# Four instead of three blocks of the up projection with seven products, and other places for the units between their steps

## The chip, the cores and the metric

The kernel runs on one core of a Trainium2 chip. The core has a matrix engine (TensorE; PE in the profile, with PEld for its weight loads), a vector engine (VectorE, DVE), a scalar engine (ScalarE, ACT), GpSimd (POOL) and SyncE (SP), each working through its own queue in order; here SP issues the loads and POOL issues the stores of the hidden layer. The metric is device time in microseconds (us) of one execution, as the median of several. Before the change it is 1566.11 us (three runs, 1565.74 to 1566.63).

## What is computed

One encoder block on 256 tokens of width 2048, in float32: a retention branch and a latent-attention branch, merged by gates and added to the residual stream, then a squared-ReLU MLP, then a last norm. The change concerns the MLP:

```python
z = _rmsnorm(h, norm_mlp_g[l]) @ w_up[l]            # 256 x 2048 times 2048 x 8192
h = h + jnp.square(jax.nn.relu(z)) @ w_down[l]      # 256 x 8192 times 8192 x 2048
```

## The kernel before, in words

**Two halves for one float32.** Each float32 operand is split into `hi`, a copy cast to fp32r by ACT, and `lo`, the remainder, which DVE gets by subtracting (`split`, L550 and L551). A product is then three matmuls: activation hi by weight hi, activation lo by weight hi, activation hi by weight lo. The activations are split once. Every weight of `w_up` is loaded by SP in pieces of 512 KB, cast by ACT, and subtracted by DVE.

**Two ways to the up projection.** The 8192 hidden columns are 64 groups of 128.

- A *unit* (class `Unit`) makes one group of 128 columns from all 2048 rows: two parts of 8 row tiles. Each part has 8 matmuls of 512 columns (L176: the activations' hi and lo halves side by side) and 8 of 256 columns (L180). Its result stands in one PSUM bank. `evict` copies it out on ACT (L1266), adds the two halves on DVE (L1267), and two parts later ACT takes the relu (L1270) and the square (L1231), and POOL stores it (L1232).
- A *block* makes 1024 columns (8 groups) in eight *steps* (class `Step`, j = 0 to 7). A step takes 256 rows by 1024 columns as a 2 by 2 arrangement of sub-blocks, and multiplies it in seven products instead of eight (`PRODUCTS`), each of three matmuls of 512 columns (L333 to L335): 21 matmuls. It has four parts, with 6, 6, 6 and 3 matmuls. Their weights are made from what was loaded: `fa` (L307), and `fb` in two adds (L316, L317), all on DVE; then part 0's weights (`ra`), part 1's (`fa`), part 2's (`fb`) and half of part 3's (`rb`) are split as above. The seven sums accumulate over the eight steps in seven PSUM banks.

At a block's end `s_end` adds the seven sums up: four copies on ACT (L522 to L528), four adds on DVE (L520) at once, and three later ones (`SUMS`), 4, 7 and 10 parts on. The result stands tokens by columns and must be turned. A *turn* (L1284) is four transposes on PE into one PSUM bank, then a relu (L1236) and a square (L1231) on ACT, and a store. A block has four turns, one at the start of part 1 of each of the next block's steps 1 to 4 (`between`). The last block's are put into two late units (`drain`).

**Banks.** There are eight PSUM banks in two rings of four (`mmps` L149, `atps` L152). During a block the seven products hold four of the one and three of the other. The fourth of the `atps` ring serves the units and the turns in turn.

**The order.** All engines follow one order written out by hand. `parts` lists the parts of steps and units. `stream` (L470) goes through it: for part n it first issues the loads up to part n + 6, then the preparation (ACT's cast, DVE's adds and subtractions) up to part n + 4, then the matmuls of part n with what follows them (a unit's `evict`, a block's `s_end`), and then what is due (`soon`). So on DVE and ACT, whatever follows the matmuls of part n stands behind the preparation of part n + 4 and ahead of that of part n + 5. Weights split by `split` live in seven slots, raw ones in five.

The first three units (`EARLY`) come before the first block, the last two (`LATE`) after the last. In the first block DVE also makes the combinations of the activations for steps 4 to 7 (`hc.make`, from part 7 and from part 24 on, `MAKE`), in four pieces each.

Where the other units stand is set by `use`, a set of (block, step, part): after such a part a unit follows.

```python
slots = [(u, j, h) for u in range(SU) for j in range(SJ) for h in (1, 3)][:-1]
whole = [t for t in slots if t[2] == 3]
room = len(units) - len(whole)
```

With three blocks there are 64 - 24 = 40 units, 35 of them between the steps. Each step but the very last is followed by one (23), and the 12 left stand in the middle, after part 1, of every second step (0, 2, 4 and 6).

The down projection then reads the hidden layer back, the units' columns first and the blocks' after, and its order follows from the number of blocks in the same way.

Of the kernel before, what the change touches and what calls it, by code (L numbers as in the profile page):

```python
# [27 lines left out]
CHUNK = 64  # L28
DFF = 8192
FT = DFF // P  # L30
SU = 3
SJ = KT // 2
ST = SU * 1024 // P
EARLY, LATE = 3, 2
AHEAD = 4
PAIRED = 6
MAKE = 7, 2 * EARLY + 18
SUMS = (4, 7, 10), (0, 1, 2)
MANUAL = {getattr(mybir.EngineType, n) for n in ('Activation', 'DVE', 'PE', 'SP', 'Pool')}
# [66 lines left out]
def block_kernel(ctx: ExitStack, tc: tile.TileContext, A):  # L106
# [50 lines left out]
    def wtile(kind, shape):  # L157
        uid[0] += 1
        dt, bufs = (F32, 5) if kind == "raw" else (F32R, 4)
        return wp.tile(shape, dt, tag=kind, bufs=bufs, name=f"{kind}{uid[0]}")  # L160
# [440 lines left out]
    for k in range(KT):  # L601
        t = lead0[:, N_VEC:] if k == 0 else wtile("raw", [P, LEAD])
# [674 lines left out]
    def turn(u, jj):  # L1277
        pT = atps(f"zt{u}{jj}")
        for j in range(2):
            kt = 2 * jj + j  # L1280
            for t in range(2):
                o = j * S + t * P
                src = zo[:, 0, 2 * t + kt // 4, kt % 4 * P : kt % 4 * P + P]
                PE.transpose(pT[:, o : o + P], src, ident)  # L1284
        square(4 * u + jj, pT)

    def step(u, j, qs):
        def end():
            sums = s_end(qs, zo[:, 0].rearrange("p (t c) n -> p t c n", t=2), zo[:, 1])
            next(sums)  # L1290
            later.extend([d, lambda: next(sums)] for d in SUMS[u == SU - 1])
            turns.extend(lambda jj=jj: turn(u, jj) for jj in range(4))
# [13 lines left out]
    early = [Unit(i, 0) for i in range(EARLY)]  # L1306
    parts = [(e, h) for h in range(2) for e in early]
    units = list(range(EARLY, FT - ST - LATE))
    slots = [(u, j, h) for u in range(SU) for j in range(SJ) for h in (1, 3)][:-1]
    whole = [t for t in slots if t[2] == 3]  # L1310
    room = len(units) - len(whole)
    halves = [t for t in slots if t[2] == 1]
    if room >= 0:
        use = set(whole) | {halves[i * len(halves) // room] for i in range(room)}
    else:
        use = {t for t in whole if t[1] != PAIRED or t[0] >= -room}
    for u in range(SU):
        qs = {}
        for j in range(SJ):
# [69 lines left out]
    def finish(half, t, c, n, lo=0, hi=512):  # L1389
        h = residual(half, t, c)[:, lo:hi]  # L1390
        ps = both[half].q[ROLE[t, c]][:, lo:hi]
        V.scalar_tensor_tensor(h, in0=ps, scalar=rh2[:, t : t + 1], in1=h, op0=ALU.mult, op1=ALU.add)

        def square():
            SC.activation(ps, h, AF.Square, accum_out=ssf[:, t, n : n + 1])

        return square
# [90 lines left out]
    with tc.manual_schedule(engines=MANUAL):  # L1488
        stream(parts, after)
        assert not later  # L1490
        for t in range(2):
            for c in range(2):
# [10 lines left out]
                else:  # L1503
                    halves = [finish(1, t, 1, 3, 0, 256)]
# [86 lines left out]
```

## Time and profile before

| what | before |
| --- | --- |
| median of three runs | 1566.11 us (1565.74 to 1566.63) |
| span of the profiled execution | 1564.8 us |
| PE, PEld busy | 1551.3 us (99%), 1311.0 us (84%) |
| DVE busy | 1316.0 us (84%) |
| ACT busy | 962.6 us (62%) |
| POOL busy | 39.3 us (3%) |
| mean granted TensorE clock | 0.998 |
| DMA | 333.70 MB, mean 213 GB/s |
| first block starts, last block ends on PE | 895.78, 1209.45 us |

The profile is of one execution, and its own time is given as the span, from the first to the last instruction; no other time is shown for that execution. The three timed runs lie 0.9 to 1.8 us above it. A row of the timeline gives start, duration, engine, line, operation, output and inputs with their shape, the count where several equal ones in a row are merged, and in brackets how long the engine had been idle before and what released it. Durations of instructions that follow each other can overlap a little, so what one costs its engine is read from start to start.

### The profile page before, as it was taken

How to read it: one execution, taken by the hardware profiler on the slowest of the kernel's cores; microseconds unless marked ns; L12 is line 12 of the kernel's file. 1: busy time of each engine (PE TensorE's matmuls, PEld its weight loads, DVE VectorE, ACT ScalarE, POOL GpSimd, SP SyncE). 2: the span in 40 equal slices, each digit the busy share in tenths (PEclk: the TensorE clock that was granted, in tenths of full speed). 3: DMA queues.
4: the chain of work that ended last, by engine and by line, in shares of the span. 5: the costliest groups of instructions: out<-in, count | busy, mean ns of one | idle time of the engine just before them, and what ended most of it. 6: DMA issues, size and time to landing. Idle time of an engine off the chain costs nothing.

```text
span 1564.8 us, 21391 instructions
## 1 busy us (share of the span) xinstructions
PE 1551.3 (99%) x7655; PEld 1311.0 (84%) x7655; DVE 1316.0 (84%) x1787; ACT 962.6 (62%) x1416; POOL 39.3 (3%) x76
## 2 busy tenths in 40 slices
PE   9999999999999999999999999999999999999997
PEld 7888888888898888888888888888888888888886
DVE  7898877799976988976567689887978899989996
ACT  6645655566545667875445567676767766656664
POOL 0000000000000000000000000000000100000000
PEclk9999999999999999999999999999999999999999
DMA  9666755566656654444556657666675977686873
GB/s 319 207 203 208 230 164 161 159 201 206 206 168 220 213 197 143 157 136 161 185 206 211 236 196 247 214 226 232 207 249 188 376 265 245 237 304 211 266 255 115
DMA packets 107626, 333.70 MB, mean 213 GB/s; under 512 B 11264, under 2 KB 12160, under 8 KB 106496
## 3 DMA queue, kind: packets, MB, share of 16 engines
q1 hardware_dynamic: 104208, 318.71, 61.1%
q0 software_dynamic: 3168, 11.54, 1.9%
q10 hardware_dynamic: 144, 2.10, 0.4%
q8 instruction: 60, 0.98, 0.3%
q14 instruction: 46, 0.38, 0.1%
HBM read 319.72 MB, written 12.58 MB: 212 GB/s over the span
## 4 chain that ended last, share of the span: by engine, by line
PE 79%; DVE 1%; issue 1%; ACT 1%; DVEq 0%; POOLq 0%; POOL 0%; ACTq 0%
PE z L176 9%; PE dn L358 7%; PE dn L359 7%; PE dn L357 7%; PE z L180 5%; PE zs L333 2%; PE zs L334 2%; PE zs L335 2%; PE mo L214 2%; PE mo L215 2%; PE mo L217 2%; PE wo L214 2%; PE wo L215 2%; PE wo L217 2%; PE gm L357 2%; PE yr L358 2%
## 5 line engine op out<-in xcount | busy, mean ns | idle before, releaser
L551 DVE TENSOR_TENSOR lo<-raw,hi 128x1024 fp32r<-128x1024 f32 (+3 forms) x214 | 232.0, 1101 | 22.7 <-ACT hi L550 22.2
L169 DVE TENSOR_TENSOR lo<-raw,hi 128x1024 fp32r<-128x1024 f32 (+1 forms) x148 | 173.2, 1171 | 89.7 <-ACT hi L168 89.6
L168 ACT CAST hi<-raw 128x1024 fp32r<-128x1024 f32 (+1 forms) x148 | 149.6, 1011 | 155.9 <-PE mo L215 44.9
L550 ACT CAST hi<-raw 128x1024 fp32r<-128x1024 f32 (+3 forms) x214 | 200.0, 953 | 55.3 <-issue 9.5
L551 DVE TENSOR_TENSOR morelo<-raw,morehi 128x1024 fp32r<-128x1024 f32 (+1 forms) x118 | 127.1, 1098 | 18.8 <-ACT morehi L550 18.3
L550 ACT CAST morehi<-raw 128x1024 fp32r<-128x1024 f32 (+1 forms) x118 | 109.1, 949 | 10.5 <-issue 3.2
L550 ACT CAST hi<-forms 128x1024 fp32r<-128x1024 f32 x70 | 73.7, 1052 | 51.2 <-DVE forms L307 28.1
L176 PE MATMUL z<-hT,morehi 128*128 128x512 f32 x408 | 101.6, 391 | 0.0
L357 PE MATMUL dn<-hi,dd 128*128 128x512 f32 x230 | 89.6, 389 | 0.0
L359 PE MATMUL dn<-hi,dd 128*128 128x512 f32 x230 | 89.5, 389 | 0.0
L358 PE MATMUL dn<-lo,dd 128*128 128x512 f32 x230 | 89.5, 389 | 0.0
L551 DVE TENSOR_TENSOR lo<-forms,hi 128x1024 fp32r<-128x1024 f32 x70 | 85.0, 1221 | 5.3 <-ACT hi L550 4.9
L176 PEld LDWEIGHTS z<-hT,morehi 128*128 128x128 f32 x408 | 74.9, 188 | 14.4
L1266 ACT COPY hs<-z 128x512 f32<-128x512 f32 x40 | 23.5, 587 | 71.2 <-PE z L180 71.1
L357 PE MATMUL dn<-morehi,dd 128*128 128x512 f32 x156 | 60.7, 389 | 0.0
L358 PE MATMUL dn<-morelo,dd 128*128 128x512 f32 x156 | 60.7, 389 | 0.0
L359 PE MATMUL dn<-morehi,dd 128*128 128x512 f32 x156 | 60.7, 389 | 0.0
L180 PEld LDWEIGHTS z<-hT,morelo 128*128 128x128 f32 x408 | 55.6, 190 | 4.0
L176 PE MATMUL z<-hT,hi 128*128 128x512 f32 x232 | 57.9, 392 | 0.0
L180 PE MATMUL z<-hT,morelo 128*128 128x256 f32 x408 | 56.9, 282 | 0.0
L307 DVE TENSOR_TENSOR forms<-raw,sraw 128x1024 f32<-128x1024 f32 x46 | 56.1, 1219 | 0.3 <-DMA raw<-w_up_s 0.3
L358 PEld LDWEIGHTS dn<-lo,dd 128*128 128x128 f32 x230 | 43.2, 188 | 9.0
(500 smaller groups left out, 4193.9 us busy)
## 6 DMA issues: line engine op xcount, KB each, us to landing
raw<-w_down SPq DMA_DIRECT2D x106, 512.0 KB, 6.0
raw<-w_up SPq DMA_DIRECT2D x80, 512.0 KB, 5.1
raw<-w_rv SPq DMA_DIRECT2D x32, 512.0 KB, 4.8
raw<-w_rg SPq DMA_DIRECT2D x32, 512.0 KB, 4.3
raw<-w_gret SPq DMA_DIRECT2D x32, 512.0 KB, 4.4
raw<-w_ret_o SPq DMA_DIRECT2D x32, 512.0 KB, 5.0
raw<-w_gmla SPq DMA_DIRECT2D x32, 512.0 KB, 4.3
raw<-w_mla_o SPq DMA_DIRECT2D x32, 512.0 KB, 3.7
```

The lines of the kernel that those rows point to most:

```text
L168: SC.copy(hi, raw)
L169: V.tensor_tensor(out=lo, in0=raw, in1=hi.bitcast(F32), op=ALU.subtract)
L176: PE.matmul(out, w[0][:, k], x.both(k0 + k), start=start and k == 0, stop=False)
L180: PE.matmul(out[:, :S], w[1][:, k], x.hi(k0 + k), start=False, stop=stop and k == n - 1)
L214: PE.matmul(out, x.hi(k0 + k, ts), w[0][:, k], start=start and k == 0, stop=False)
L215: PE.matmul(out, x.lo(k0 + k, ts), w[0][:, k], start=False, stop=False)
L217: PE.matmul(out, x.hi(k0 + k, ts), w[1][:, k], start=False, stop=stop and k == nk - 1)
L357: PE.matmul(q, ah, wh, start=start, stop=False)
L358: PE.matmul(q, ah, wl, start=False, stop=False)
L359: PE.matmul(q, al, wh, start=False, stop=self.left[f] == 0)
L550: SC.copy(hi, val)
L551: V.tensor_tensor(out=lo, in0=val, in1=hi.bitcast(F32), op=ALU.subtract)
```

## The change

`SU` goes from 3 to 4: four blocks (4096 columns) instead of three are done with seven products, and 32 groups instead of 40 as units. The slots are replaced: in each block a unit stands after part 1 of steps 1 to 6, and one after the last part of step 7, but for the last block. That makes 4 x 6 + 3 = 27 units between the steps, beside the three early and the two late ones. Within a block, steps 0 and 7 have no unit in their middle, and no unit stands between two steps.

```diff
-SU = 3
+SU = 4
 SJ = KT // 2
 ST = SU * 1024 // P
...
-PAIRED = 6
...
-    slots = [(u, j, h) for u in range(SU) for j in range(SJ) for h in (1, 3)][:-1]
-    whole = [t for t in slots if t[2] == 3]
-    room = len(units) - len(whole)
-    halves = [t for t in slots if t[2] == 1]
-    if room >= 0:
-        use = set(whole) | {halves[i * len(halves) // room] for i in range(room)}
-    else:
-        use = {t for t in whole if t[1] != PAIRED or t[0] >= -room}
+    use = {(u, j, 1) for u in range(SU) for j in range(1, SJ - 1)} | {(u, SJ - 1, 3) for u in range(SU - 1)}
     for u in range(SU):
         qs = {}
         for j in range(SJ):
             st = step(u, j, qs)
             for h in range(4):
                 parts.append((st, h))
                 if (u, j, h) in use:
                     un = Unit(units.pop(0), 0)
                     parts += [(un, 0), (un, 1)]
```

`ST`, the number of groups done in blocks, follows from `SU`, and with it the layout of the two forms of `w_up`, and the order in which the down projection takes the hidden columns.

## The prediction

> **What bounds the kernel now.** I read the page's totals first, then the stretch in which the up projection runs, block by block (a block is 1024 hidden columns, done in eight steps), then who waits for whom there, and last the rows of single instructions.
>
> ```profile
> span 1564.8 us, 21391 instructions
> PE 1551.3 (99%) x7655; PEld 1311.0 (84%) x7655; DVE 1316.0 (84%) x1787; ACT 962.6 (62%) x1416; POOL 39.3 (3%) x76
> PEclk9999999999999999999999999999999999999999
> ```
>
> TensorE is busy 99% of the span, at full granted clock. By the totals, fewer matmuls are less time. But the totals are an average, so I looked at the stage itself: the columns are stretch, length, then busy us (instructions) of PE, PEld, DVE, ACT and POOL, clock, DMA share, GB/s.
>
> ```profile
> 895.78:995.34 99.56, 99.56 (x522) 85.62 (x521) 86.57 (x99) 67.53 (x95) 7.78 (x14) 1.00 0.63 216
> 1000.90:1105.16 104.26, 104.26 (x554) 89.65 (x553) 86.75 (x96) 70.37 (x101) 8.68 (x16) 1.00 0.66 219
> 1105.16:1209.45 104.29, 104.29 (x555) 89.65 (x553) 86.37 (x97) 71.25 (x102) 8.68 (x16) 1.00 0.65 218
> ```
>
> PE never stops, DVE is already busy 83 to 87%. Where its rest lies:
>
> ```profile
> ACT hs L1266 <- PE z L180: 69.3, 34, 3.6
> DVE hs L1267 <- ACT hs L1266: 26.9, 19, 2.8
> DVE morelo L551 <- ACT morehi L550: 14.1, 21, 1.6
> ```
>
> Once per unit ACT waits for PE to finish it (L1266), and DVE waits for ACT (L1267). Both queues are in order, so they cannot prepare further than four parts beyond the unit that PE is in. DVE's free time cannot be saved up: that is the point of the whole forecast.
>
> **The change part by part. PE's saving.** The rows of PE around the end of the first block and in the next:
>
> ```profile
> 990.55 0.40 PE L333 MATMUL zs<-hi,hT 128*128 128x512 f32 x1
> ...
> 995.34 1.98 PE L176 MATMUL z<-hT,morehi 128*128 128x512 f32 x8
> ...
> 1000.90 0.40 PE L333 MATMUL zs<-morehi,hT 128*128 128x512 f32 x1
> ...
> 1009.21 0.40 PE L333 MATMUL zs<-hi,hc 128*128 128x512 f32 x1
> ...
> 1011.27 1.98 PE L176 MATMUL z<-hT,morehi 128*128 128x512 f32 x8
> ...
> 1016.83 0.40 PE L333 MATMUL zs<-hi,hT 128*128 128x512 f32 x1
> ...
> 1022.12 1.98 PE L176 MATMUL z<-hT,morehi 128*128 128x512 f32 x8
> ```
>
> A step is 990.55 to 995.34, 4.79 us for 21 matmuls (0.228 each). A unit is 995.34 to 1000.90, 5.56. Parts 2 and 3 of a step (9 matmuls) are 1009.21 to 1011.27, 2.06. A step with a turn (four transposes ahead of part 1) is 5.29, so a turn costs 0.50. The change takes out eight units and puts in eight steps and four turns: 8 x 5.56 - 8 x 4.79 - 4 x 0.50 = 4.2 us saved, all of it on the path, if PE stays fed. Bytes are the same (1 MB for a unit or a step).
>
> **What DVE is asked for.** The end of the first block on DVE:
>
> ```profile
> 991.37 0.43 DVE L1267 TENSOR_TENSOR hs<-hs 128x256 f32<-128x256 f32 x1 [0.66 <-ACT hs L1266]
> 992.32 2.36 DVE L551 TENSOR_TENSOR morelo<-raw,morehi 128x1024 fp32r<-128x1024 f32 x2 [0.52 <-ACT morehi L550]
> 994.60 1.22 DVE L307 TENSOR_TENSOR forms<-raw,sraw 128x1024 f32<-128x1024 f32 x1
> ...
> 998.20 1.22 DVE L551 TENSOR_TENSOR lo<-forms,hi 128x1024 fp32r<-128x1024 f32 x1
> 999.34 2.14 DVE L520 TENSOR_TENSOR zo<-zs,zo 128x512 f32<-128x512 f32 x3
> ...
> 1001.99 2.35 DVE L551 TENSOR_TENSOR lo<-raw,hi 128x1024 fp32r<-128x1024 f32 x2
> 1004.26 0.42 DVE L1267 TENSOR_TENSOR hs<-hs 128x256 f32<-128x256 f32 x1
> 1004.60 1.22 DVE L551 TENSOR_TENSOR lo<-forms,hi 128x1024 fp32r<-128x1024 f32 x1
> 1005.73 0.68 DVE L551 TENSOR_TENSOR morelo<-raw,morehi 128x512 fp32r<-128x512 f32 x1
> 1006.33 0.68 DVE L520 TENSOR_TENSOR zo<-zo 128x512 f32<-128x512 f32 x1
> ```
>
> From start to start: a split of 1024 takes 1.14, one of 512 0.60, part 0 of a step 3.60 (994.60 to 998.20), the four sums at a block's end 2.65, each later sum 0.61, a unit's add 0.34. So a step costs DVE 3.60 + 1.14 + 1.14 + 0.60 = 6.48 against PE's 4.79; a unit 2.27 + 0.34 = 2.61 against 5.56. Only units feed DVE's slack. Eight steps with seven units and 4.5 of sums make 74.6 on DVE, 78.8 on PE (with four turns): 95% instead of 83 to 87. On average that fits. What matters is where units stand: between the unit in step 6 and the one in step 1 of the next block lie two and a half steps with one unit, and the sums.
>
> **The boundary, summed along the queues.** T is the end of step 6's unit on PE. The rows of ACT that price its part:
>
> ```profile
> 990.75 0.59 ACT L1266 COPY hs<-z 128x512 f32<-128x512 f32 x1 [1.38 <-PE z L180]
> 991.24 2.00 ACT L550 CAST morehi<-raw 128x1024 fp32r<-128x1024 f32 x2
> 993.14 0.41 ACT L1270 ACTIVATE hs<-hs 128x256 f32<-128x256 f32 x1
> ...
> 993.91 1.04 ACT L550 CAST morehi<-sraw 128x1024 fp32r<-128x1024 f32 x1
> ...
> 1001.58 1.05 ACT L550 CAST hi<-forms 128x1024 fp32r<-128x1024 f32 x1
> 1002.53 0.62 ACT L550 CAST morehi<-raw 128x512 fp32r<-128x512 f32 x1
> ...
> 1029.31 0.62 ACT L550 CAST morehi<-raw 128x512 fp32r<-128x512 f32 x1
> 1029.83 0.60 ACT L1236 ACTIVATE hs<-zt 128x512 f32<-128x512 f32 x1
> ```
>
> ACT's copy starts at T + 0.20 and takes 0.49; a cast takes 0.95, a short one 0.52, a unit's relu and square 0.77, a turn's relu 0.60. DVE's first split after the wait starts at T + 1.77 (992.32 less 990.55). Then: parts 2 and 3 of step 7, 1.74; 0.5 of waiting, since ACT has the old unit's relu and square ahead of the next cast; the end unit 2.27; parts 0 and 1 of the next step 0, 4.74; sums 2.65; its parts 2 and 3, 1.74; the end unit's add 0.34; the first add (L307) of step 1, 1.14. That is T + 16.9. On that add ACT waits, and then has in its queue: cast 0.95, relu and square 0.77, two unit casts 1.90, two casts of step 1 1.47, and the relu of turn 0, 0.60: T + 22.7 with 0.1 of hand-over.
>
> Who waits for that relu: the units and the turns share one PSUM bank. Seven products hold seven of eight (four of L149, three of L152), so the unit in step 1 cannot start until the turn before it is read out. PE undisturbed would start it at T + 2.06 + 4.79 + 5.56 + 4.79 + 3.2 (part 0, turn, part 1) = T + 20.4. **Loss 2.3 us, at three boundaries 6.9.** Two smaller waits on the way (part 0's and part 1's lo of step 1, about 0.4 and 0.6) are contained in it. Bounds: if ACT's chain had slack that I miss, only those two remain, 1.0 each boundary; if DVE reaches T a step's part late, 4.
>
> **Turn and unit in one step.** The same bank in steps 2 to 4: ACT has after the unit's copy two unit casts, relu and square, two step casts and then the turn's relu: 0.20 + 0.49 + 1.90 + 0.77 + 0.95 + 0.52 + 0.60 = T + 5.43; PE wants the bank at T + 5.29. With the hand-over 0.25, nine times: **2.2 us** (bounds 0 and 5). Before, the turn's relu followed closer on a unit's copy (1029.83), and no bank wait appears.
>
> **The first block.** It has no turns, but the activations' combinations of steps 4 to 7 are made in it (groups by form: count, busy us, mean ns, idle before):
>
> ```profile
> L231 DVE TENSOR_TENSOR raw<-hT 128x1024 f32<-128x1024 f32 x2 | 2.4, 1218 | 0.0
> L237 DVE TENSOR_TENSOR raw<-raw 128x256 f32<-128x256 f32 x2 | 0.8, 418 | 0.0
> L551 DVE TENSOR_TENSOR hc<-raw,hc 128x1024 fp32r<-128x1024 f32 x2 | 2.4, 1219 | 0.0
> ```
>
> and its start on PE and on DVE:
>
> ```profile
> 895.78 0.40 PE L333 MATMUL zs<-morehi,hT 128*128 128x512 f32 x1
> ...
> 896.63 0.42 DVE L1267 TENSOR_TENSOR hs<-hs 128x256 f32<-128x256 f32 x1
> ```
>
> Each of two makings costs 2 x 1.14 + 4 x about 0.39 = 3.8. From 896.97, DVE does step 1's parts 0 and 1 (4.74 and 0.2 of waiting), its unit, the first making's start 1.14, parts 2 and 3 with 0.67 of making, step 2's part 0 with 0.89, its part 1: 913.3. PE wants that at 895.78 + 4.79 + 2.73 + 5.56 + 2.06 + 1.37 + 0.46 = 912.7. Carried on, the second making leaves DVE at 945.6 against PE's 944.5 in step 5. **Loss 1.8 us** (0 to 4). The tail (last block, late units) keeps its order of units and sums: nothing, 0 to 1.
>
> **Sum.** -4.2 + 6.9 + 2.2 + 1.8 = +6.7 on the span, 1571.5. The timed median, 1566.11, lies 1.3 above the span of 1564.8, which I keep: **1572.9 us, 0.43% slower**. Bounds of the terms together: -4.2 + 3 = 1564.9 to -4.2 + 22 = 1583.9, both unlikely at once.
>
> **The rivals.** *PE's saving stays* (faster): DVE and ACT have the hidden room that the average of 95% allows, waits vanish because lo is wanted only at a part's third matmul; 1566.1 - 4.2 + 1 = about 1563. For it: no PE wait in the stage now, with s_end's sums already 4 us late (999.34 against PE's 995.34). Against: the chain of 16.9 has no idle time in it. *The losses cancel the gain* (no change): boundaries at 1.0 instead of 2.3 give 1566.1 - 4.2 + 3 + 1 + 1 = about 1567. *DVE saturates* (slower still): each of 27 units keeps some 1 us of its present wait (26.9 over 19, the L1267 row, is 1.4) on top of 95%: 4 x (74.6 + 7) against 4 x 78.8 on PE, +11 less the 4.2, about 1573 to 1580; it decides if DVE never recovers within a block.
>
> *The clock falls*: PEclk is 1.00 in every stretch above, and there is no PE gap in them to learn from. My gaps are pieces of 0.4 to 1.3 us. If one stretch after a gap ran at half clock, fifteen matmuls of 0.228 would take 3.4 us longer. At three boundaries that makes 1583. The Trainium skill, "TensorE: Matmul & The Clock Gate", section "Why this matters for your kernels", warns of gaps over some 3 us; by that rule pieces this short keep the clock, and no run here shows a longer one in this stage.
>
> The bank wait has a rule of its own, which speaks against this change: the Trainium skill, "Perfetto Trace Analysis", section "Optimization Strategy", says that the same gap repeating on the engine that should be saturated can mean that PSUM has no room for the next tile. By it the nine gaps of 0.25 should be alike; the sum stays the same.
>
> **How the numbers follow.** Forecast 0.50, saturated DVE 0.09, clock 0.03 (slower, 0.62 in all); cancelled 0.20 (within 0.2%, some 3 us, about what these runs can tell from no change); saving stays 0.18 (faster). The range runs from 1562 (the saving whole) to 1579 (boundaries at 4). The forecast's own is 1569.5 to 1577.
>
> **What would show it.** In the changed kernel's waits PE should appear in this stage: z (L176) waiting for ACT's relu of the turn, three times about 1 us and nine times about 0.2; zs waiting for DVE's lo in step 1. DVE should be over 93% busy between the early and the late units; that stretch should last 313.7 + 6.7 = 320 us. The forecast is wrong if PE shows no wait there, or if the stretch is under 312.

## The result and the profile after

The changed kernel takes 1574.51 us (median of four runs, 1574.05 to 1574.96) against 1565.92 (four runs, 1565.62 to 1566.63): ratio 1.0053, 95% interval 1.0040 to 1.0065. It is slower by 8.6 us. The profiled execution took 1574.36, with a span of 1572.6, 7.8 more than the span before. One constant is gone from the head of the file, so lines stand one lower than before (L1266 is now L1265).

The page's totals after:

```profile
span 1572.6 us, 21298 instructions
PE 1552.4 (99%) x7583; PEld 1303.2 (83%) x7583; DVE 1349.0 (86%) x1826; ACT 970.1 (62%) x1420; POOL 37.0 (2%) x72
PEclk9999999999999999999999999999999999999999
```

There are 72 matmuls fewer, and PE is busy for about as long. The page of the profile alone would not tell that anything is wrong: PE still shows 99%. The stage does. First the whole stretch before, from the first step to the first late unit; then, after, the first block (up to the unit behind its step 7) and the whole stretch (columns as in the prediction):

```profile
895.78:1209.45 313.67, 313.67 (x1659) 269.82 (x1657) 265.15 (x297) 214.04 (x304) 25.14 (x46) 1.00 0.65 219
```

```profile
895.13:969.50 74.37, 72.23 (x362) 60.88 (x361) 72.04 (x84) 51.38 (x70) 5.05 (x9) 1.00 0.66 214
...
895.13:1217.25 322.12, 314.74 (x1586) 262.01 (x1585) 298.52 (x336) 222.29 (x309) 22.87 (x42) 1.00 0.64 213
```

The stretch grew from 313.67 to 322.12, by 8.45 us. That is the whole loss: from the first late unit to the first matmul of the down projection it is 12.8 both times, and from there to the end 342.5 both times. (The spans differ by less, 7.8, because in the profiled execution before the stretch began 0.65 later.) DVE is busy 92.7% of the stretch instead of 84.5%, in the first block 97%, and PE now has gaps, at full clock. Who waits, from the waits of the changed kernel in and around this stretch (total us, times, longest), for PE's matmuls and for its weight loads:

```profile
PE zs L334 <- DVE lo L550: 3.6, 6, 1.6
PE z L175 <- ACT hs L1235: 2.9, 3, 1.0
PE zs L334 <- DVE morelo L550: 0.7, 2, 0.4
PEld z L175 <- ACT hs L1235: 8.3, 12, 1.4
```

Before, PE had no wait here. Now the weight loads of twelve units wait for ACT's relu of a turn (L1235), that is, for the PSUM bank that units and turns share (the bank, from here on): three long, nine short ones. Eight waits are for DVE's lo, the remainder half of split weights. The matmuls' own waits count only 7.2 us, since a matmul counts as busy until its modelled end; what a wait costs must be read from start to start. The end of the first block on PE:

```profile
962.67 0.40 PE L332 MATMUL zs<-hi,hc 128*128 128x512 f32 x1
...
969.50 1.98 PE L175 MATMUL z<-hT,hi 128*128 128x512 f32 x8
...
980.81 0.50 PE L334 MATMUL zs<-lo,hT 128*128 128x512 f32 x1 [0.35 <-DVE lo L550]
...
983.28 0.50 PE L334 MATMUL zs<-lo,hc 128*128 128x512 f32 x1 [0.37 <-DVE lo L550]
...
985.44 2.11 PE L175 MATMUL z<-hT,hi 128*128 128x512 f32 x8 [0.97 <-ACT hs L1235]
...
991.13 0.40 PE L332 MATMUL zs<-morehi,hc 128*128 128x512 f32 x1
...
996.59 2.09 PE L175 MATMUL z<-hT,hi 128*128 128x512 f32 x8
```

T, the end of step 6's unit, is 962.67; 969.50 is the start of the end unit, the one behind step 7. The unit of the next step 1 starts at 985.44, T + 22.8 instead of the T + 20.4 of an undisturbed PE. The next one starts 5.46 after the end of the unit before it (991.13 to 996.59), not 5.29, and those units take 5.69 instead of 5.56 (985.44 to 991.13). The queues behind that boundary on DVE, and on ACT:

```profile
973.68 2.14 DVE L519 TENSOR_TENSOR zo<-zs,zo 128x512 f32<-128x512 f32 x3
...
978.40 1.22 DVE L306 TENSOR_TENSOR forms<-raw,sraw 128x1024 f32<-128x1024 f32 x1
```

```profile
979.71 1.05 ACT L549 CAST hi<-forms 128x1024 fp32r<-128x1024 f32 x1 [2.92 <-DVE forms L306]
980.67 0.41 ACT L1269 ACTIVATE hs<-hs 128x256 f32<-128x256 f32 x1
...
981.44 1.99 ACT L549 CAST hi<-raw 128x1024 fp32r<-128x1024 f32 x2
983.32 1.06 ACT L549 CAST morehi<-forms 128x1024 fp32r<-128x1024 f32 x1
984.27 0.62 ACT L549 CAST morehi<-raw 128x512 fp32r<-128x512 f32 x1
984.79 0.60 ACT L1235 ACTIVATE hs<-zt 128x512 f32<-128x512 f32 x1
```

ACT sits idle for 2.92 us until DVE has done the first add of step 1, then works without a gap through one cast of the step, the end unit's relu and square, two unit casts and two more casts of the step, and only then reads out the turn's bank, until 985.39; PE goes on at 985.44.

### The profile page after: what moved, and what is told of

It reads as the page before. It is cut to its first block, busy times and chain, and to the rows that moved or that the text cites. A ratio compares the mean times of both kernels' runs of the same rounds, so it can differ in the third digit from the quotient of the medians.

```text
span 1572.6 us, 21298 instructions
## 1 busy us (share of the span) xinstructions
PE 1552.4 (99%) x7583; PEld 1303.2 (83%) x7583; DVE 1349.0 (86%) x1826; ACT 970.1 (62%) x1420; POOL 37.0 (2%) x72
## 4 chain that ended last, share of the span: by engine, by line
PE 72%; DVE 4%; ACT 3%; issue 2%; DMA 0%; DVEq 0%; POOLq 0%; POOL 0%; ACTq 0%
PE dn L356 7%; PE dn L358 7%; PE dn L357 7%; PE z L175 6%; PE z L179 3%; PE zs L334 2%; PE zs L332 2%; PE zs L333 2%; PE mo L213 2%; PE mo L214 2%; PE mo L216 2%; PE wo L213 2%; PE wo L214 2%; PE wo L216 2%; PE gm L358 2%
## 5 line engine op out<-in xcount | busy, mean ns | idle before, releaser
L550 DVE TENSOR_TENSOR lo<-raw,hi 128x1024 fp32r<-128x1024 f32 (+3 forms) x238 | 254.7, 1086 | 30.2 <-ACT hi L549 29.7
L549 ACT CAST hi<-raw 128x1024 fp32r<-128x1024 f32 (+3 forms) x238 | 219.5, 941 | 59.1 <-PE yr L358 6.4
L550 DVE TENSOR_TENSOR morelo<-raw,morehi 128x1024 fp32r<-128x1024 f32 (+1 forms) x86 | 91.3, 1077 | 6.0 <-ACT morehi L549 5.9
L549 ACT CAST morehi<-raw 128x1024 fp32r<-128x1024 f32 (+1 forms) x86 | 78.9, 933 | 7.1 <-issue 2.1
L549 ACT CAST morehi<-forms 128x1024 fp32r<-128x1024 f32 x51 | 53.6, 1052 | 45.7 <-DVE forms L306 27.5
L175 PE MATMUL z<-hT,hi 128*128 128x512 f32 x312 | 79.0, 395 | 2.1 <-ACT hs L1235 1.9
L550 DVE TENSOR_TENSOR lo<-forms,hi 128x1024 fp32r<-128x1024 f32 x57 | 69.6, 1221 | 4.1 <-ACT hi L549 3.4
L175 PEld LDWEIGHTS z<-hT,hi 128*128 128x128 f32 x312 | 56.5, 188 | 16.1 <-ACT hs L1235 5.5
L550 DVE TENSOR_TENSOR morelo<-forms,morehi 128x1024 fp32r<-128x1024 f32 x51 | 62.3, 1221 | 2.5 <-ACT morehi L549 2.0
L358 PEld LDWEIGHTS dn<-hi,dd 128*128 128x128 f32 x240 | 45.0, 188 | 9.5
L356 PEld LDWEIGHTS dn<-hi,dd 128*128 128x128 f32 x240 | 45.1, 188 | 9.3
```

Of the source, the lines that this page charges most:

```text
L175: PE.matmul(out, w[0][:, k], x.both(k0 + k), start=start and k == 0, stop=False)
L356: PE.matmul(q, ah, wh, start=start, stop=False)
L358: PE.matmul(q, al, wh, start=False, stop=self.left[f] == 0)
L549: SC.copy(hi, val)
L550: V.tensor_tensor(out=lo, in0=val, in1=hi.bitcast(F32), op=ALU.subtract)
```

## The experiments

All times are medians beside runs of the kernel before on the same chip (1565.92 in the first four, 1565.95 in the others); what is gained or lost against the changed kernel is counted from its 1574.51, taken beside 1565.92.

**Four blocks with the old places.** The old kernel with one number changed:

```diff
-SU = 3
+SU = 4
```

> Four blocks as in the changed kernel, but the 27 units stand where the old rule puts them: one after the last part of every step but step 6 (and but the very last step). My theory (the places of the units make the loss: DVE's queue at a block's boundary and the PSUM bank that turn and unit share): no unit follows a turn within its step, so no bank waits; at the boundary DVE is about 1 us late (sums 4.74 + 6.48 + 2.27 behind the last unit), the first block has a unit after step 0 and no wait. -4.2 + 3 x 1.0 + 0.5 against the kernel before: about 1565 us, PE's waits in the stage about 3 to 4 us. Rival (DVE is simply too full with four blocks, wherever units stand): as slow as the changed kernel, 1573 to 1576.

Measured 1569.33 us, ratio 1.0022 (1.0013 to 1.0031): 4 us above my figure and 4 below the rival's, so neither was right. The places do matter: the new ones cost 5 us beside the old ones, and four blocks do not pay in the old places either. PE's waits there:

```profile
PE zt L1284 <- ACT hs L1266: 2.1, 3, 0.7
PE zs L335 <- DVE morelo L551: 2.1, 4, 0.9
PE zs L335 <- DVE lo L551: 0.2, 1, 0.2
```

I had named the bank but only looked for units that wait for a turn. Here it is the other way round: turn 0 stands only six matmuls behind the unit that closes step 0, and waits until ACT has copied that unit out, since ACT's queue is late at the boundary:

```profile
988.00 0.66 PE L1284 MATMUL zt<-con,zo 128*128 128x128 f32 x4 [0.70 <-ACT hs L1266]
```

And the first block, which I had put at 0.5, has two of the waits for DVE, of 0.9 while the combinations are made and of 0.7 in step 7, which follows step 6 without a unit between them.

**Turns behind the unit.**

```diff
-            if part == 1:
+            if part == 3:
                 self.between()
```

> The changed kernel with each turn ahead of part 3 of its step instead of part 1, that is behind the unit and not ahead of it. My theory: the nine small bank waits (0.29 each with their restart) vanish, 2.6 us; at each boundary the unit of step 1 no longer waits for the relu of turn 0, but DVE's lo of step 1 is still late, by 0.4 and about 1.0, so that 0.9 of 2.5 is gained, three times 2.7: about 1574.5 - 5.3 = 1569 us, no wait of z for ACT's L1235 left. Rival (DVE too full): the bank waits only take up time that PE would spend on waiting for DVE; 1573 to 1575.

Measured 1569.62 us, 1.0025 (1.0016 to 1.0034). The units' waits for a turn's relu are gone, all twelve; what is left on the matmuls is DVE:

```profile
PE zs L334 <- DVE lo L550: 4.5, 6, 1.7
PE zs L334 <- DVE morelo L550: 1.1, 2, 0.8
```

4.9 us gained of 5.3 expected. The lo waits at a boundary went from 0.35 and 0.37 to 0.35 and 0.80: the turn, 0.50 long, no longer stands ahead of the second one and covers part of it. From start to start a boundary still costs 1.7 of the 2.5 us: from the end of the end unit (975.51) to the unit in step 1 (984.76) PE takes 9.25 us, and undisturbed it would take 7.52. So at a boundary most of the loss is DVE's lateness, and the bank adds 0.7 to 0.8.

**No making in the first block.** The kernel leaves out the combinations of the activations for steps 4 to 7: these steps read those of steps 0 to 3 instead, and DVE is spared the two makings.

```diff
-            o = self.t[j // 4][:, j % 4]
+            o = self.t[0][:, j % 4]
...
-        elif n in MAKE:
-            making = hc.make(2 + MAKE.index(n))
```

> The changed kernel without the making of the activations' combinations for steps 4 to 7: steps 4 to 7 multiply by those of steps 0 to 3 (that part of the computation is left out). Nothing else is changed. My theory: PE's two waits in the first block (0.8 in step 2, 1.9 in step 5) vanish with the 2 x 3.8 us of DVE, 2.7 us less, 1571.8 us; the boundaries and the bank waits stay. Rival (the first block is late because step 0 has no unit in its middle, the making does not matter): 1574 to 1575, the waits of step 2 and step 5 stay.

Measured 1571.82 us (1570.87 to 1571.86), 1.0035 (1.0022 to 1.0048): 2.7 less, as expected. Both waits of the first block are gone, and the rest is as in the changed kernel:

```profile
PE z L175 <- ACT hs L1235: 2.8, 3, 0.9
PE zs L334 <- DVE lo L550: 1.4, 4, 0.4
PE zs L334 <- DVE morelo L550: 0.7, 2, 0.4
```

**Units one step earlier.**

```diff
-    use = {(u, j, 1) for u in range(SU) for j in range(1, SJ - 1)} | {(u, SJ - 1, 3) for u in range(SU - 1)}
+    use = {(u, j, 1) for u in range(SU) for j in range(SJ - 2)} | {(u, SJ - 1, 3) for u in range(SU - 1)}
```

> The changed kernel with the units of the inner steps after part 1 of steps 0 to 5 instead of 1 to 6; the end units stay. My theory: DVE starts each block's sums at T + 17 against PE's T + 11.6 and is not later to part 0 of the next block than before the change, and the unit in step 0 (no turn ahead of it, so no bank wait) covers the preparation of step 1: a boundary costs 0.3 to 0.5 instead of 2.5, the first block 0 to 0.5 instead of 2.7; the bank waits become twelve of 0.29, 3.5. -4.2 + 1.2 + 0.3 + 3.5: about 1566.5 to 1567 us. Rival (DVE too full): the wait moves to steps 6 and 7, which have no unit, and the time stays at 1572 to 1576.

Measured 1572.52 us, 1.0041 (1.0028 to 1.0053): a miss by 5.5 us. The time is within the rival's figure, but its wait in steps 6 and 7 did not come, except for one of 0.4 in the first block; the other lo waits went. The bank took their place at step 1, worse than before (three of 1.66 to 1.69). Why, on DVE, on ACT and on PE:

```profile
985.54 0.41 DVE L1266 TENSOR_TENSOR hs<-hs 128x256 f32<-128x256 f32 x1
```

```profile
983.07 0.57 ACT L1265 COPY hs<-z 128x512 f32<-128x512 f32 x1
983.55 2.00 ACT L549 CAST morehi<-raw 128x1024 fp32r<-128x1024 f32 x2
985.99 0.42 ACT L1269 ACTIVATE hs<-hs 128x256 f32<-128x256 f32 x1 [0.45 <-DVE hs L1266]
...
988.22 0.59 ACT L1235 ACTIVATE hs<-zt 128x512 f32<-128x512 f32 x1
```

```profile
988.86 1.43 PE L175 MATMUL z<-hT,morehi 128*128 128x512 f32 x5 [1.66 <-ACT hs L1235]
```

I had counted step 1 as a steady step. But DVE is still behind from the sums, so ACT copies the unit of step 0 late (983.07; PE had finished it at 981.76), waits for DVE's add of it before it may take its relu, and reaches the turn late.

**ACT's order alone.** A unit's own relu and square come two parts later, behind a turn's relu in the steady steps. No work is moved off DVE.

```diff
-            later.append([2, rest])
+            later.append([4, rest])
```

> The changed kernel with one number changed: a unit's own relu and square are due 4 instead of 2 parts after its copy, so that on ACT they stand behind the next turn's relu. The turns stay ahead of part 1. My theory (ACT's order sets when the shared bank is read out): the relu of a turn comes 0.77 earlier, T + 4.7 against PE's want at T + 5.3, so the nine small waits vanish (2.6 us with restarts), and at a boundary the chain is 0.8 shorter on ACT and 0.5 on DVE (the first cast of the end unit): 1.3 of 2.5 gained, three times 3.9: about 1568 us. Rival (only DVE's amount of work matters, the order on ACT does not): no work is moved off DVE, 1574 to 1575.

Measured 1569.88 us, 1.0025 (1.0015 to 1.0034): 4.6 less than the changed kernel, where I had said 6.5 and the rival none. The nine short waits are gone. The three long ones stayed, at 0.9, because there the end unit's relu (L1269) still stands ahead of the turn's (L1235):

```profile
PE zs L334 <- DVE lo L550: 2.8, 4, 1.8
PE z L175 <- ACT hs L1235: 2.7, 3, 0.9
```

```profile
982.17 0.41 ACT L1269 ACTIVATE hs<-hs 128x256 f32<-128x256 f32 x1
...
984.39 0.58 ACT L1235 ACTIVATE hs<-zt 128x512 f32<-128x512 f32 x1
```

I had forgotten that the end unit stands six parts ahead of turn 0, so that four parts do not put its relu behind it. The boundary gained 0.55 instead of 1.3: end unit to unit of step 1 is 969.64 to 985.03 here, 969.50 to 985.44 in the changed kernel.

**More sums.**

```diff
-        tt(V, c11, q5, f)
+        for _ in range(3):
+            tt(V, c11, q5, f)
```

> The changed kernel with the fourth sum at each block's end done three times (the result is the same): 1.2 us more on DVE at each of four boundaries. My theory (the chain from step 6's unit to turn 0's relu has no slack): PE's wait grows by 1.2 at three boundaries, 3.6 in all, nothing at the last: about 1578 us. Rival (the queues have slack there, the loss is in the steady steps): 1574.5 to 1575.

Measured 1579.62 us, 1.0085 (1.0071 to 1.0098): 5.1 more. DVE's row gives the size that I had too low:

```profile
976.19 2.14 DVE L519 TENSOR_TENSOR zo<-zo 128x512 f32<-128x512 f32 x3
978.24 1.22 DVE L551 TENSOR_TENSOR morelo<-forms,morehi 128x1024 fp32r<-128x1024 f32 x1
```

The sum takes 2.05 instead of 0.60, 1.45 more, three times 4.35; a wait of 0.3 before the first late turn is new, too (I had put nothing at the last block). Together that is 4.7 of the 5.1. The stretch lasts 326.55, 4.43 more than in the changed kernel: what DVE is given at a boundary comes out on PE in full, so that chain has no slack.

**Both remedies: units earlier and turns behind them.** The edits of the second and the fourth experiment.

> Four blocks, the inner units after part 1 of steps 0 to 5 and the turns ahead of part 3. Units shifted alone took the lo waits away but left twelve bank waits (three of 1.8, nine of 0.2, with restarts some 8.5 us). My theory: with the turn behind the unit these vanish, and the unit in step 0 covers step 1's preparation, so no lo wait takes their place: 1572.5 - 8.5 = 1564 us, that is 1.5 to 2.5 below the kernel before, PE's waits in the stage under 2 us. Rival (the bank waits only hid DVE's lateness, as they did in part when the turns alone were moved): lo waits of about 1.4 at each boundary come back, 1568 to 1569.

Measured 1565.79 us (1564.43 to 1566.53), 0.9997 (0.9988 to 1.0005): no difference from the kernel before that can be told, 1.8 above my figure and 2 to 3 below the rival's. In the profiled execution the stretch lasted 312.02, 1.65 less than before, but at 1564.73 that execution is one of the shorter ones. Nearly all waits of the matmuls are gone. What was left of them in and behind the stretch, and the weight loads' waits for the same copy:

```profile
PE zt L1283 <- ACT hs L1265: 0.3, 2, 0.2
PE zs L334 <- DVE morelo L550: 0.3, 1, 0.3
PE zt L1283 <- ACT morehi L549: 0.2, 1, 0.2
...
PEld zt L1283 <- ACT hs L1265: 1.7, 3, 0.6
```

At each boundary turn 0 waits a little for the copy of step 1's unit, which ACT does late, behind a cast that waited for DVE:

```profile
992.16 1.05 ACT L549 CAST hi<-forms 128x1024 fp32r<-128x1024 f32 x1 [3.13 <-DVE forms L306]
993.11 0.58 ACT L1265 COPY hs<-z 128x512 f32<-128x512 f32 x1
```

**And the later sums put off.** As the last one, and:

```diff
-SUMS = (4, 7, 10), (0, 1, 2)
+SUMS = (13, 16, 19), (0, 1, 2)
```

> As shifted_late, with the three later sums of a block due 13, 16 and 19 parts on instead of 4, 7 and 10: 1.8 us of DVE leave the crowded stretch. My theory: if shifted_late has no lo wait left at a boundary there is nothing to gain, within 0.5 us of it. Rival (DVE's lateness still shows there): up to 3 x 0.6 us faster.

Measured 1563.95 us (1562.60 to 1564.43), 0.9985 (0.9977 to 0.9994): 1.8 less than without, as the rival said, and 2.0 less than the kernel before. The stretch, and the waits of PE's matmuls in it and just behind it (the second stands before the first late turn):

```profile
895.21:1205.99 310.78, 310.38 (x1586) 262.98 (x1585) 295.28 (x335) 221.62 (x307) 22.86 (x42) 1.00 0.66 219
...
PE zs L334 <- DVE morelo L550: 0.4, 1, 0.4
PE zt L1283 <- DVE zo L519: 0.2, 1, 0.2
```

310.78 is 2.9 below the 313.67 of before. With DVE busy 95%, more than in the changed kernel, PE has lost nearly all its waits. The saving of 4.2 is real, and 2.9 of it are kept in the stretch; 0.4 go again behind it, where the first late unit and the down projection are now 13.25 apart instead of 12.8. No other kernel here is faster.

## Why the prediction was right

**Direction and size.** Forecast 1572.9 with 1562 to 1579, measured 1574.51. The time alone would also fit *DVE saturates* (1573 to 1580). That the forecast case and not this rival is what happened is seen in the stage: the stretch was to last 320 us and lasted 322.1; three long and nine short waits for the turn's relu were to appear, and did; DVE was to be over 93% busy and was 92.7%, just under. And in steps 5 to 7 of the later blocks PE has no wait (none between 1018.87 and 1063.40, for one), so DVE does recover within a block.

**PE's saving.** The sum of the measured gaps from start to start is 2.7 in the first block (74.37 less 8 x 4.79 and 6 x 5.56), 7.4 at the three boundaries and 2.6 in nine steady steps, 12.7 together, where the forecast had 6.9 + 2.2 + 1.8 = 10.9: each of the three terms was somewhat too small. The stretch grew by 8.45. So 4.2 were saved, as worked out. (The gaps are counted against the lengths of before; units without a wait still have them, as 924.15 to 929.71, 5.56.)

**The boundary.** The chain was right to 0.1 us, at its end and on the way, so it was no luck that it came out: the sums start at T + 11.0 in both (973.68), first add of step 1 done at T + 16.9 (979.62 less 962.67 is 16.95), turn's relu read out at T + 22.7 (985.39: 22.72). The loss was 2.5 for 2.3 each; the missing 0.1 to 0.2 is the start after a wait, in which the unit takes 5.69 instead of 5.56, and which the sum had left out. That the relu and DVE's work in front of it set the loss is shown by the turns moved, by ACT's order alone, and by the longer sums. The bounds' lower case, 1.0 a boundary, was set too low: with the bank out of the way (turns behind the unit) the lo waits cost 1.7.

**Turn and unit in one step.** T + 5.43 was forecast for the relu; measured 5.41:

```profile
995.95 0.59 ACT L1235 ACTIVATE hs<-zt 128x512 f32<-128x512 f32 x1
```

which ends at 996.54, T being 991.13. Each costs 0.29 with its restart (0.25 in the sum), nine times 2.6 for 2.2. The experiment on ACT's order took these away without touching DVE's work.

**The first block** is the term that was mis-sized most: 2.7 for 1.8. It waits in step 2 and step 5, as forecast (0.5 and 1.6 in the rows, 0.8 and 1.9 with restarts). They were to be 0.6 and 1.1. What the second has more is mostly a row that the sum did not have, and with it the wait of SP's queue that lies behind it:

```profile
939.71 1.23 DVE L306 TENSOR_TENSOR forms<-raw,sraw 128x1024 f32<-128x1024 f32 x1 [0.77 <-DMA raw<-w_up_s]
```

```profile
SPq L300 <- DVE raw L236: 8.5, 1, 8.5
```

DVE stands still 0.77 us for a load. The makings hold two of the five raw slots, so half of step 5's weights can be fetched only when another slot is free: SP held this load back 8.5 us for DVE and issued it at 934.62, as DVE ended the first split of the unit in step 4 (at 934.59). The row names the instruction behind it, one of the making (L236, from 934.51); which of the two frees the slot it does not settle. Without the makings these loads wait under 0.3 us for DVE, and DVE does not wait for one. That the makings are the cause of both waits is shown by leaving them out; that within this it is the slots, and not only DVE's time, is read from these rows, and no run gave the makings slots of their own.

**The rivals.** *PE's saving stays* and *The losses cancel the gain* fell with the time and with the waits. *DVE saturates* fell as a rival of its own: with nearly the same DVE work (295.28 us busy against 298.52) in a stretch shorter by 11 us, the last experiment has nearly no waits. It is not the amount of DVE's work but what stands in its queue, and in ACT's, ahead of a bank that PE needs. *The clock falls*: PEclk stayed at 1.00 through gaps of up to 1.6 us in the rows, and of 1.8 in the experiment on ACT's order; none longer was seen in this stage. The Trainium skill, "TensorE: Matmul & The Clock Gate", section "Why this matters for your kernels", warns of gaps over some 3 us, and these traces agree as far as they go. The rule of the repeating gap in the Trainium skill, "Perfetto Trace Analysis", section "Optimization Strategy", pointed at the right place: twelve units waited for one PSUM bank. The same bank was enough, though, once the order was changed (last experiment).

**Where my theory failed** was in the expectations of the experiments, mostly at one point: I took the step after a boundary for a steady one. There ACT is late for the copy of a unit, too, and the bank makes the turn wait for the unit (old places, both remedies) or the unit for the turn (units shifted). And I held that without a lo wait the later sums were free. They cost 1.8 us by the medians; by the rows all three stand ahead of the add that ACT's cast waits for, and behind that cast stands the copy.

## What to carry to other kernels

When an engine that is not the bound is ordered by hand together with others, compare its work with the bound's between two fixed points of the order (here from unit to unit), not over the stage: with DVE busy 95% on average PE lost 1.3 us in one order, and with DVE busy 93% it lost 12.7 us in another. A buffer that two users share can put everything in the reader's queue ahead of its read on the critical path; moving the user, or what stands before the read, was a change of one number here and gave back 4.9 and 4.6 us. Count gaps on a pipelined engine from start to start: PE's rows of waits showed 7.2 of 12.7 us.

## What the runs showed that was not expected

A gap on PE costs more than its wait: the first matmul after one takes 0.50 instead of 0.39, and a unit begun after a wait takes 5.69 instead of 5.56. From start to start, waits of 0.35, 0.51 and 1.63 in the rows cost 0.63, 0.80 and 1.92. On DVE a sum that writes the same place again starts 0.72 after the one before, where the instruction behind the last of them starts after 0.61: three took 2.05, where I had reckoned with 1.8.
